# Attention row sums inverted on GpSimd by a power of minus one, and the convolution's first tap moved to ScalarE

## The chip, the cores and the metric

The kernel runs on one core of a Trainium2 chip. A core has a matrix engine (TensorE, PE in the profile, with its weight loads as PEld), VectorE (DVE), ScalarE (ACT), GpSimd (POOL) and SyncE (SP), which here issues nearly all DMAs. Each engine works through its own instruction list in order, and they wait for each other by semaphores. The metric is the device time of one execution in microseconds (us); lower is better.

## The reference

One layer of a hybrid encoder: sequence 1024, width 1024, float32. The input is normalised and modulated, projected once, and the columns go to two groups of heads: axial-rotary attention (8 heads of 64, two key/value heads) and a bidirectional mLSTM (4 heads of 128). Both are joined by an output projection; a SwiGLU feed-forward layer and a last norm follow. What the change touches is the softmax of the attention and the convolution ahead of the mLSTM:

```python
def one_block(q_blk):
    s = jnp.einsum('bkgqd,bksd->bkgqs', q_blk, kt).astype(jnp.float32) * scale
    p = jax.nn.softmax(s, axis=-1).astype(vt.dtype)
    return jnp.einsum('bkgqs,bksd->bkgqd', p, vt)

def centred_depthwise_conv(x, w, b):          # x: (B, S, 1024), width 5
    y = lax.conv_general_dilated(x, w[:, None, :], (1,), [(2, 2)],
            dimension_numbers=('NWC', 'WIO', 'NWC'), feature_group_count=ch)
    return y + b

qk = jax.nn.silu(centred_depthwise_conv(qk_pre, conv_w, conv_b))
```

## The kernel before, in words

**Precision.** PE multiplies rounded float32 operands. To keep accuracy every operand is split into a high part (rounded, on ACT) and a low part (the rest, a subtraction on POOL or DVE); a product is three matmuls (`mm3`, lines 298 to 300). Weights come by DMA into `wst`, and `whi` (ACT) and `wlo` (POOL) are made from them.

**Order.** All orders are fixed when the program is built. A planner (`Clock`) holds an estimated cost of every instruction and simulates the engines; `Clock.chain` runs a list of steps one behind the other, each when its predecessor is done by the estimate plus a delay, and an instruction is written into its engine's list at the moment the planner gets to it. All elementwise instructions go out through `Engine.emit`, so nearly all of them carry line 96 in the profile, and tile names tell them apart. In a chain, `bg` names for a step an engine that it waits to find free in the plan before it is issued. The planner prices a DVE `reciprocal` of one column at 0.07 us, a GpSimd `pow` at 0.1 us plus 0.21 per element and partition, a DVE `tensor_scalar` of 1024 with two column operands at 0.80, an ACT activation of that size with column scale and bias at 1.13 us.

**Streams.** PE's work is written as generators. In the attention stage the main ones are `values`, `turned` and `scores`; whenever none of them can go on in the plan, PE takes a step of the projection units (`units(IN)`), among them eight `conv_unit`s. Units that aren't done by the end of attention go on during the mLSTM stage.

**Attention.** There are 64 blocks (8 heads, 8 query tiles of 128). For one block:

- `scores` (line 978): PE makes S, 128 queries by 1024 keys, in PSUM (two buffers).
- `top`: DVE takes the row maximum into column 0 of the small tile `sst` and scales it into column 1.
- `exp`: ACT writes P (three buffers) in SBUF, with the row sum accumulated into column 2 (this ends with an ACTIVATION_READ_ACCUMULATOR).
- DVE's `reciprocal` writes column 3 of `sst`.
- `norm`: POOL multiplies P by that column, in place.
- `turned` (line 1010): PE transposes P in two halves into the PSUM tile T (two buffers); ACT copies the high part to PT, DVE subtracts the low part into PT.
- `values` (line 1029): for two blocks at a time PE multiplies PT by the values into `av`; ACT and DVE add its two halves (`avt`), and SP stores them.

**Queries.** Each head's queries are loaded (`qd`) and split into `qs` (ACT, then POOL).

**Convolution.** A `conv_unit` projects 128 channels of 1024 positions into `acc`, ACT copies them to `xp` (two zeros on each side), and then a chain runs: `tap(0)` makes `y` from `xp`, weight column and bias; `tap(1)` to `tap(4)` add the other shifted products on DVE; ACT's tanh and one DVE instruction make the SiLU; SP stores `y` to DRAM for the mLSTM. Between them DVE also takes the products for the modulation vector (`ada`).

Of the kernel before, what the change touches and what calls it, by code (L numbers as in the profile page):

```python
# [11 lines left out]
F32 = mybir.dt.float32  # L12
F32R = mybir.dt.float32r
BF16 = mybir.dt.bfloat16
AF = mybir.ActivationFunctionType
OP = mybir.AluOpType
# [4 lines left out]
P = 128  # L21
S = 1024
# [14 lines left out]
LAT = 0.14  # L37
# [203 lines left out]
def layer_kernel(ctx, tc, xT, c, w_ada, vecs, cons, rope, w_f, w_t0, w_t, w_o, w_gu, w_d, out):  # L241
    nc = tc.nc

    const = ctx.enter_context(tc.tile_pool(name="const", bufs=1))
# [5 lines left out]

    both = const.tile([P, 2], F32, name="both")
    mhalf, eps = both[:, 0:1], both[:, 1:2]
    nc.vector.memset(mhalf, -0.5)
    nc.vector.memset(eps, EPS)
    vec = const.tile([P, NVEC], F32, name="vec")
    nc.scalar.dma_start(vec, vecs)
# [3 lines left out]
    def V(n, i=0, w=1):  # L260
        o, _ = VEC[n]
        return vec[:, o + i:o + i + w]
# [39 lines left out]
    def dma(dst, src, q=None):  # L302
        (q or nc.sync).dma_start(dst, src)
        on_chip = dst.space == src.space == bass.MemoryType.SB if hasattr(src, "space") else False
        return ck.dma(math.prod(dst.shape) * 4, 0.65 if on_chip else 0.5)

    def halves(n):
        return slice(n * HALF, (n + 1) * HALF)

    ck = Clock()  # L310
    dve, act, gps = Engine(ck, nc.vector, "dve"), Engine(ck, nc.scalar, "act"), Engine(ck, nc.gpsimd, "gps")
# [28 lines left out]
    def psum_tile(shape, tag):  # L340
        t, bufs = PP["tags"][tag]
        f = Flag()
        PP["ring"].setdefault(t, []).append(f)
        return PP["ps"].tile(shape, F32, tag=t, name=tag, bufs=bufs), f
# [6 lines left out]
    with tc.manual_schedule():  # L351
# [351 lines left out]
        def tile_mms(w0, last):  # L703

            for n in range(NH):
                for k in range(KT):
                    yield [pieces[w0 + k // 4][2]] + ([slot("acc")] if k == 0 else [])
                    if k == 0:
                        acc, f = psum_tile([P, HALF], "acc")
                        open_sum[0] = True  # L710
                    mm3(acc, weights(w0, k, 4), (h_hi[k][:, halves(n)], h_lo[k][:, halves(n)]), k == 0, k == KT - 1)
                    ck.pe(0.65)
                    if n == 1 and k % 4 == 3:
                        load_piece()
                    if k == KT - 1:
                        open_sum[0] = False
                        last(n, acc, f)
# [13 lines left out]
        def conv_unit(i, w0):  # L731
            yield convs[-2:-1]
            prev = convs[-1:] if nbig[0] < 4 else []
            convs.append(mqk_ok[i])
            xp = bp.tile([P, S + 4], F32, tag="big", name="xp")
            gps.memset(xp[:, 0:2], 0.0)
            gps.memset(xp[:, S + 2:S + 4], 0.0)
            Y = []

            def tap(j):  # L740
                if j == 0:
                    Y.append(bp.tile([P, S], F32, tag="big", name="y"))
                    dve.tensor_scalar(Y[0], xp[:, 0:S], V("conv_w", i * 5), V("conv_b", i), op0=OP.mult, op1=OP.add)
                else:
                    dve.scalar_tensor_tensor(
                        Y[0], xp[:, j:j + S], V("conv_w", i * 5 + j), Y[0], op0=OP.mult, op1=OP.add)

            def tanh():
                act.activation(xp[:, 0:S], Y[0], AF.Tanh, scale=0.5)

            def silu():

                dve.scalar_tensor_tensor(Y[0], xp[:, 0:S], 1.0, Y[0], op0=OP.add, op1=OP.mult)

            def store():
                dma(mqk_d[i], Y[0])

            def last(n, acc, f):
                def evac():
                    act.activation(xp[:, 2 + n * HALF:2 + (n + 1) * HALF], acc, AF.Copy)  # L760

                e = ck.chain(LAT, evac, flag=f)
                if n == 1:
                    eng = ["dve"] * 5
                    ck.chain(LAT, e, *prev, *[lambda j=j: tap(j) for j in range(5)], tanh, silu, store,
                             flag=mqk_ok[i], bg=[None] * (1 + len(prev)) + eng + ["act", "dve", None])

            yield from tile_mms(w0, last)

        mqk_ok = [Flag() for _ in range(8)]  # L770
# [165 lines left out]
        def ada_late(last=48, ahead=2):  # L936

            n = len(adas)
            if n == 64 and all(f.done for f in adas[-2:]) and not summed:
                summed.append(1)  # L940
                mod_sum(40, 48)
            if n >= last or n >= ahead and not (adas[n - ahead].done and adas[n - ahead].t <= ck.t):
                return
            j, i = 16 + n // 2, n % 2
            t = PP["ada"].tile([P, HALF], F32, tag="ada", name="ada", bufs=ahead)
            adas.append(ck.chain(dma(t, w_ada[j][:, halves(i)]), lambda: dve.scalar_tensor_tensor(
                t, t, 1.0, PP["cond"][:, halves(i)], op0=OP.mult, op1=OP.mult, accum_out=modacc[:, i, j:j + 1])))
# [4 lines left out]
        Pok = [Flag() for _ in range(NQ)]  # L952
# [4 lines left out]
        def att_q(h):  # L957
            qd = ap.tile([P, S], F32, tag="qd", name="qd", bufs=1)
            src = q_d[h // 2][(h % 2) * DH:(h % 2 + 1) * DH]
            dma(qd[0:DH], src)  # L960
            arrive = dma(qd[DH:P], src)
            qs = ap.tile([P, S], F32R, tag="qs", name="qs")
            Q[h] = qs, ck.chain(arrive, lambda: act.activation(qs, qd, AF.Copy),
                                lambda: gps.tensor_sub(qs[DH:P], qd[DH:P], qs[DH:P].bitcast(F32)))

        def scores():

            for q in range(NQ):
                h, j = divmod(q, NJ)
                if j == 2 and h + 1 < AH:  # L970
                    att_q(h + 1)
                ada_late()
                g, (qs, ok) = h // 4, Q[h]
                yield [ok, k2_ok[g]] + [slot("S")] + Tem[max(q - 3, 0):max(q - 2, 0)]
                sp, f = psum_tile([P, S], "S")
                for n in range(NH):
                    for m in range(2):
                        nc.tensor.matmul(sp[:, halves(n)], qs[:, j * P:(j + 1) * P], k2[g][m][:, halves(n)],  # L978
                                         start=m == 0, stop=m == 1)
                ck.pe(0.87)  # L980
                st = ap.tile([P, 4], F32, tag="sst", name="sst", bufs=6)
                cq = colq[:, j, h:h + 1]

                def top(st=st, sp=sp, cq=cq):
                    dve.reduce_max(st[:, 0:1], sp, axis=AX.X)
                    dve.tensor_scalar(st[:, 1:2], st[:, 0:1], cq, -1.0, op0=OP.mult, op1=OP.mult)

                def exp(st=st, sp=sp, cq=cq, q=q, f=f):
                    Pt[q] = ap.tile([P, S], F32, tag="P", name="P", bufs=3)
                    act.activation(Pt[q], sp, AF.Exp, bias=st[:, 1:2], scale=cq, accum_out=st[:, 2:3])  # L990
                    f.set(ck, ck.fin + LAT)

                def norm(st=st, q=q):
                    gps.tensor_scalar(Pt[q], Pt[q], st[:, 3:4], 0.0, op0=OP.mult, op1=OP.add)

                ck.chain(LAT, top, exp, lambda st=st: dve.reciprocal(st[:, 3:4], st[:, 2:3]), norm, flag=Pok[q])

        def turned():

# [44 lines left out]
        Y = {}  # L1044
# [893 lines left out]
        psum_open("ps1", {"acc": ("acc", 1), "acct": ("acc", 1), "T": ("T", 2), "S": ("S", 2), "av": ("av", 1)})  # L1938
        att_q(0)
        ck.streams([Stream(values()), Stream(turned()), Stream(scores())], [un])  # L1940
        ck.streams([un], stop=lambda: convs[-1].done and len(convs) == 8 and not open_sum[0])
        while len(adas) < 48:
# [144 lines left out]
```

## Time and profile before

| what | value |
|---|---|
| median of 3 runs | 1405.1 us (1402.33 to 1405.69) |
| the profiled execution | 1407.29 us |
| its span, first to last instruction | 1405.5 us |
| mean granted TensorE clock | 0.972 |
| attention blocks, first maximum to last average | about 209 to 507 us |
| first taps of the eight convolutions | first at 191.1 us, last at 460.1 us |

The profile is of one execution. Busy time is given by engine; a group of instructions is one engine, operation and pair of tiles, with its count, busy time, mean in ns, the idle time of the engine just before it and what ended that. A wait is put down to whatever ended it last. "issue" is a wait for which the profile shows no cause. In time order a row gives start, duration, engine, line, operation and tiles, and in brackets the idle time before it.

### The profile page before, as it was taken

How to read it: one execution, taken by the hardware profiler on the slowest of the kernel's cores; microseconds unless marked ns; L12 is line 12 of the kernel's file. 1: busy time of each engine (PE TensorE's matmuls, PEld its weight loads, DVE VectorE, ACT ScalarE, POOL GpSimd, SP SyncE). 2: the span in 40 equal slices, each digit the busy share in tenths (PEclk: the TensorE clock that was granted, in tenths of full speed). 3: DMA queues.
4: the chain of work that ended last, by engine and by line, in shares of the span. 5: the costliest groups of instructions: out<-in, count | busy, mean ns of one | idle time of the engine just before them, and what ended most of it. 6: DMA issues, size and time to landing. Idle time of an engine off the chain costs nothing.

```text
span 1405.5 us, 19481 instructions
## 1 busy us (share of the span) xinstructions
PE 1300.5 (93%) x6594; PEld 1072.1 (76%) x6602; DVE 1065.1 (76%) x1600; ACT 662.9 (47%) x1194; POOL 679.0 (48%) x555
## 2 busy tenths in 40 slices
PE   5789798999999989899996999999999999979997
PEld 2578577889878979777774888888888887757887
DVE  7947979986788848768589886666666654798866
ACT  5454316677666655454476333332332334344463
POOL 5555554545344336577421355454544545545542
PEclk9899989999999999999998999999999999989999
DMA  7446462322122146553552333322332259723324
GB/s 287 165 128 203 135 172 80 108 77 65 38 65 70 35 140 211 188 203 115 196 187 75 113 120 105 107 104 100 110 113 90 71 175 327 275 81 102 93 65 154
DMA packets 103172, 184.40 MB, mean 131 GB/s; under 512 B 11296, under 2 KB 32672, under 8 KB 103072
## 3 DMA queue, kind: packets, MB, share of 16 engines
q1 hardware_dynamic: 89968, 161.06, 36.0%
q10 hardware_dynamic: 13104, 22.10, 4.2%
q8 instruction: 52, 0.85, 0.2%
q14 instruction: 48, 0.39, 0.1%
HBM read 136.19 MB, written 43.25 MB: 128 GB/s over the span
## 4 chain that ended last, share of the span: by engine, by line
PE 61%; DVE 20%; DMA 6%; issue 5%; ACT 3%; POOL 3%; SPq 1%; DVEq 0%; ACTq 0%; POOLq 0%
PE acc L299 15%; PE acc L298 15%; PE acc L300 15%; DVE x L96 3%; PE av L1029 3%; DVE ada L96 3%; DVE sst L96 2%; PE T L1010 2%; DVE PT L96 2%; PE S L978 2%; DVE y L96 1%; PE acct L298 1%; PE acct L300 1%; PE acct L299 1%; DVE wd L96 1%
## 5 line engine op out<-in xcount | busy, mean ns | idle before, releaser
L96 POOL TENSOR_TENSOR wlo<-wst,whi 128x512 fp32r<-128x512 f32 (+2 forms) x196 | 279.5, 1432 | 285.0 <-ACT whi L96 272.9
L96 ACT ACTIVATE whi<-wst 128x512 fp32r<-128x512 f32 (+2 forms) x219 | 131.0, 605 | 125.1 <-POOL wlo L96 25.3
L96 POOL TENSOR_SCALAR P<-P,sst 128x1024 f32<-128x1024 f32 x64 | 88.9, 1392 | 141.1 <-DVE sst L96 106.4
L299 PE MATMUL acc<-x,whi 128*128 128x512 f32 x352 | 140.7, 400 | 5.9 <-DVE x L96 5.9
L96 POOL TENSOR_TENSOR wlo<-wr,whi 128x512 fp32r<-128x512 f32 x56 | 76.9, 1374 | 77.4 <-ACT whi L96 73.9
L298 PE MATMUL acc<-hh,whi 128*128 128x512 f32 x224 | 97.5, 435 | 14.1 <-ACT hh L96 11.8
L298 PE MATMUL acc<-whi,wch 128*128 128x512 f32 x244 | 97.2, 398 | 6.3 <-ACT wch L96 6.3
L96 ACT ACTIVATE P<-S,sst,colq 128x1024 f32<-128x1024 f32 x64 | 77.3, 1207 | 52.4 <-DVE sst L96 47.9
L299 PE MATMUL acc<-hl,whi 128*128 128x512 f32 x224 | 92.4, 412 | 8.2 <-POOL hl L96 4.5
L300 PE MATMUL acc<-whi,wcl 128*128 128x512 f32 x244 | 97.2, 398 | 2.9 <-DVE wcl L96 2.8
L299 PE MATMUL acc<-wlo,wch 128*128 128x512 f32 x244 | 97.0, 398 | 0.6 <-POOL wlo L96 0.5
L96 DVE SCALAR_TENSOR_TENSOR ada<-ada,cond 128x512 f32<-128x512 f32 (+1 forms) x79 | 80.2, 1023 | 18.3 <-DMA ada<-in_w_ada_dram 12.7
L300 PE MATMUL acc<-hh,wlo 128*128 128x512 f32 x224 | 91.5, 409 | 0.0
L96 DVE TENSOR_TENSOR sg<-acc,sg 128x512 f32<-128x512 f32 x67 | 45.4, 687 | 58.8 <-PE acc L300 58.5
L96 ACT ACTIVATE PT<-T 128x512 fp32r<-128x512 f32 x128 | 71.4, 597 | 37.7 <-PE T L1010 36.9
L96 ACT ACTIVATE whi<-wr 128x512 fp32r<-128x512 f32 x60 | 37.9, 632 | 108.1 <-DVE wr L96 50.3
L96 DVE TENSOR_TENSOR PT<-T,PT 128x512 fp32r<-128x512 f32 x128 | 82.8, 681 | 7.2 <-ACT PT L96 7.1
L96 POOL TENSOR_TENSOR wlo<-s,whi 128x512 fp32r<-128x512 f32 x40 | 53.8, 1347 | 70.7 <-ACT whi L96 70.7
L299 PEld LDWEIGHTS acc<-x,whi 128*128 128x128 f32 x352 | 67.0, 190 | 22.3 <-DVE x L96 7.3
L298 PE MATMUL acct<-whi,hh 128*128 128x256 f32 (+1 forms) x256 | 79.4, 310 | 2.5 <-ACT xp L96 1.2
L96 DVE TENSOR_TENSOR wcl<-wd,wch 128x512 fp32r<-128x512 f32 x50 | 48.0, 972 | 42.1 <-ACT wch L96 26.9
L1010 PE MATMUL T<-con,P 128*128 128x128 f32 x512 | 70.3, 275 | 10.2 <-DVE PT L96 7.4
(459 smaller groups left out, 3802.5 us busy)
## 6 DMA issues: line engine op xcount, KB each, us to landing
wr<-in_w_gu_dram SPq DMA_DIRECT2D x66, 256.0 KB, 2.8
ada<-in_w_ada_dram SPq DMA_DIRECT2D x64, 256.0 KB, 3.3
wd<-in_w_d_dram SPq DMA_DIRECT2D x22, 512.0 KB, 7.0
wst<-in_w_gu_dram SPq DMA_DIRECT2D x34, 256.0 KB, 3.1
wst<-act_d SPq DMA_DIRECT2D x33, 256.0 KB, 4.1
ada<-in_w_ada_dram SPq DMA_DIRECT2D x16, 512.0 KB, 5.5
wst<-in_w_o_dram SPq DMA_DIRECT2D x32, 256.0 KB, 4.3
act_d<-sg ACTq DMA_DIRECT2D x31, 256.0 KB, 2.0
```

The lines of the kernel that those rows point to most:

```text
L96: return fn(*args, **kw)
L298: nc.tensor.matmul(acc, w[0], x[0], start=first, stop=False)
L299: nc.tensor.matmul(acc, w[0], x[1], start=False, stop=False)
L300: nc.tensor.matmul(acc, w[1], x[0], start=False, stop=last)
L978: nc.tensor.matmul(sp[:, halves(n)], qs[:, j * P:(j + 1) * P], k2[g][m][:, halves(n)], start=m == 0, stop=m == 1)
L1010: nc.tensor.transpose(tp[:, k], Pt[q][:, (4 * b + k) * P:(4 * b + k + 1) * P], ident)
L1029: nc.tensor.matmul(av, va[:, k, h // 4], PT[it][m][:, k], start=(k, m) == (0, 0), stop=(k, m) == (NJ - 1, 1))
```

## The change

A constant column of minus ones is made once. In the convolution, `tap(0)` is an ACT activation (identity, with the weight column as scale and the bias column as bias) in place of DVE's `tensor_scalar`, and in the chain it waits in the plan for ACT to be free instead of DVE. In the attention, the step between `exp` and `norm` is a GpSimd `tensor_tensor` that raises the row sum to the power of minus one, in place of DVE's `reciprocal`. As the planner prices the new instructions differently, the orders that it writes for all engines can differ from there on.

```diff
     both = const.tile([P, 2], F32, name="both")
     mhalf, eps = both[:, 0:1], both[:, 1:2]
+    mone = const.tile([P, 1], F32, name="mone")
     nc.vector.memset(mhalf, -0.5)
+    nc.vector.memset(mone, -1.0)
     nc.vector.memset(eps, EPS)
...
                 if j == 0:
                     Y.append(bp.tile([P, S], F32, tag="big", name="y"))
-                    dve.tensor_scalar(Y[0], xp[:, 0:S], V("conv_w", i * 5), V("conv_b", i), op0=OP.mult, op1=OP.add)
+                    act.activation(Y[0], xp[:, 0:S], AF.Identity, scale=V("conv_w", i * 5), bias=V("conv_b", i))
...
                 if n == 1:
-                    eng = ["dve"] * 5
+                    eng = ["act"] + ["dve"] * 4
...
-                ck.chain(LAT, top, exp, lambda st=st: dve.reciprocal(st[:, 3:4], st[:, 2:3]), norm, flag=Pok[q])
+                ck.chain(LAT, top, exp, lambda st=st: gps.tensor_tensor(st[:, 3:4], st[:, 2:3], mone, op=OP.pow),
+                         norm, flag=Pok[q])
```

## The prediction

> **What bounds the kernel now.** I read the page first, then the busy time by stretches, then what TensorE (PE) waits for in the attention stage, since both edits act only there. The page:
>
> ```profile
> span 1405.5 us, 19481 instructions
> PE 1300.5 (93%) x6594; PEld 1072.1 (76%) x6602; DVE 1065.1 (76%) x1600; ACT 662.9 (47%) x1194; POOL 679.0 (48%) x555
> ```
>
> PE is the busiest engine. The stretches 190 to 510 us hold all attention blocks and all eight convolutions (columns: PE, PEld, DVE, ACT, POOL busy, then granted clock, DMA share, GB/s):
>
> ```profile
> core 0: us, PE busy (x) PEld busy (x) DVE busy (x) ACT busy (x) POOL busy (x), PEclk, DMA share, GB/s
> 190.00:510.00 320.00, 302.63 (x1957) 263.85 (x1957) 269.29 (x448) 203.00 (x353) 140.51 (x104) 1.00 0.25 74
> 200.00:300.00 100.00, 90.89 (x569) 77.72 (x568) 95.77 (x162) 63.89 (x107) 51.13 (x33) 1.00 0.37 111
> 300.00:400.00 100.00, 98.17 (x650) 86.26 (x650) 72.97 (x132) 68.15 (x121) 42.46 (x39) 1.00 0.20 56
> 400.00:510.00 110.00, 104.31 (x703) 92.75 (x704) 90.89 (x145) 68.72 (x122) 43.27 (x31) 1.00 0.15 47
> ```
>
> PE is idle for 320.00 - 302.63 = 17.4 us. Nearly all of it lies where VectorE (DVE) is full: 9.1 us in 200:300 at 96% DVE, against 1.8 us in 300:400 at 73%. While attention is held up, PE does projection matmuls of the next units; a faster attention chain only moves those matmuls later, so PE's 302.6 us are work that stays. What a change here can win is at most the 17.4 us. Who owns them:
>
> ```profile
> engine line waited for: us in total, times, longest us
> PE T L1010 <- DVE PT L96: 7.4, 9, 2.0
> PE acc L298 <- ACT xp L96: 2.2, 4, 0.7
> PE T L1010 <- POOL P L96: 1.7, 4, 0.9
> PE S L978 <- ACT P L96: 1.4, 1, 1.4
> PE acct L298 <- ACT xp L96: 1.2, 1, 1.2
> PE av L1029 <- DVE PT L96: 1.0, 2, 0.5
> PE acct L298 <- DVE avt L96: 0.9, 1, 0.9
> ```
>
> 7.4 + 1.0 + 0.9 = 9.3 us wait for a DVE evacuation of PSUM (the low half of the transposed probabilities, PT, or the sum avt). 1.7 + 1.4 = 3.1 us wait for the softmax chain, where DVE's maximum and reciprocal stand. The reason shows in time order in the worst stall, DVE and POOL (GpSimd) first, then PE:
>
> ```profile
> 434.41 0.80 DVE L96 TENSOR_SCALAR y<-xp,vec 128x1024 f32<-128x1024 f32 x1
> 435.25 2.02 DVE L96 SCALAR_TENSOR_TENSOR y<-xp,vec,y 128x1024 f32<-128x1024 f32 x1
> 437.19 0.15 DVE L96 RECIPROCAL sst<-sst 128x1 f32<-128x1 f32 x1
> 437.59 3.02 DVE L96 SCALAR_TENSOR_TENSOR y<-xp,vec,y 128x1024 f32<-128x1024 f32 x1
> 440.53 0.68 DVE L96 TENSOR_TENSOR PT<-T,PT 128x512 fp32r<-128x512 f32 x1
> ...
> 436.36 3.16 POOL L96 TENSOR_TENSOR qs<-qd,qs 64x1024 fp32r<-64x1024 f32 x1
> ...
> 441.35 0.63 PE L1010 MATMUL T<-con,P 128*128 128x128 f32 x4 [2.03 <-DVE PT L96]
> ```
>
> Three convolution taps stand in DVE's queue ahead of PT, one of them 3.02 us long beside a POOL subtraction, and PE stops for 2.03 us. The order is fixed in the program; the stall is the real DVE lagging behind the planned one.
>
> **Part 1, what DVE loses.** The rows of what is removed and of what stays around it:
>
> ```profile
> L96 DVE TENSOR_SCALAR y<-xp,vec 128x1024 f32<-128x1024 f32 x8 | 8.7, 1090 | 2.2 <-ACT xp L96 2.2
> L96 DVE SCALAR_TENSOR_TENSOR y<-xp,vec,y 128x1024 f32<-128x1024 f32 x32 | 49.3, 1541 | 0.3
> L96 DVE SCALAR_TENSOR_TENSOR y<-xp,y 128x1024 f32<-128x1024 f32 x8 | 9.7, 1214 | 0.6 <-ACT xp L96 0.6
> L96 DVE RECIPROCAL sst<-sst 128x1 f32<-128x1 f32 x64 | 10.1, 158 | 24.8 <-ACT P L96 24.7
> ```
>
> 8 x 1.090 = 8.7 us of first taps and 64 x 0.158 = 10.1 us of reciprocals go: DVE falls from 269.3 to about 250 us. Besides, at 24 of the reciprocals DVE stood still until the exponential came, 24.7 us in all; that place in DVE's queue is gone. How much of the 9.3 us of PE's waits for DVE follows is not in the trace: 0 if the redrawn order spends the room on something else, 12.4 (9.3 + 3.1) if all goes. One wait is on average 7.4 / 9 = 0.82 us; a tap ahead of it is worth 0.8 to 1.1, a reciprocal 0.16. But a convolution is (8.7 + 49.3 + 9.7) / 8 = 8.5 us of DVE, and only 1.1 of that goes, so a backlog with taps two to five in it stays a backlog. I take a little under half of 9.3: **-4.0 us**.
>
> **Part 2, the reciprocal on POOL.** No trace row has a one-element power; the two nearest have 4 and 16 elements a partition (min/median/max ns):
>
> ```profile
> L96 POOL TENSOR_TENSOR ss<-ss,both x8: 1008/1012/1381, 546.6 to 667.1; 128x4 f32<-128x4 f32 x8
> L96 POOL TENSOR_TENSOR rqv<-rqv,both x4: 2920/3242/3349, 99.7 to 179.9; 128x16 f32<-128x16 f32 x4
> ```
>
> (2920 - 1008) / 12 = 159 ns an element, so 1008 - 3 x 159 = 0.53 us for one; bounds 0.1 (no fixed cost at all) and 1.0 (all fixed). I take 0.53, the line through both. 64 x 0.53 = 34 us take POOL from 140.5 to 174 of 320 us, 54%. On the chain a short-cut and a detour meet. Where DVE is free the old step cost 0.16 and a hop, and the new one is some 0.3 us longer; where DVE is behind, the old one waited for it. The start of attention shows the second:
>
> ```profile
> 203.45 1.98 DVE L96 TENSOR_SCALAR y<-xp,vec 128x1024 f32<-128x1024 f32 x1 [0.81 <-ACT xp L96]
> 205.47 3.52 DVE L96 SCALAR_TENSOR_TENSOR y<-xp,vec,y 128x1024 f32<-128x1024 f32 x2
> 208.91 1.21 DVE L96 TENSOR_REDUCE sst<-S 128x1 f32<-128x1024 f32 x1
> ...
> 211.58 0.19 ACT L96 ACTIVATION_READ_ACCUMULATOR P<-S,sst,colq 128x1 f32 x1
> ...
> 212.86 0.16 DVE L96 RECIPROCAL sst<-sst 128x1 f32<-128x1 f32 x1
> ...
> 213.12 2.58 POOL L96 TENSOR_SCALAR P<-P,sst 128x1024 f32<-128x1024 f32 x2 [2.98 <-DVE sst L96]
> ...
> 214.65 1.09 PE L1010 MATMUL T<-con,P 128*128 128x128 f32 x8 [0.94 <-POOL P L96]
> ```
>
> The sum is there at 211.77, the reciprocal waits 1.09 us for a tap. The power would end at about 211.80 + 0.53 and the product start at 212.36 instead of 213.12: 0.76 us off the 0.94 that PE waits. The second convolution's first tap there (1.98 us, stretched) becomes an ACT instruction; its end moves between 0.78 us earlier (start 203.45, 1.24 us long, next tap at 205.47 before) and 0.2 later (behind two weight copies). I take -0.3. Opening: **-1.0 us**. At the other blocks the detour costs nothing that I count: PE waited for a product only 4 times in 64, 1.7 us in all, because the transposes stand later in PE's order, behind other matmuls. If that cover were gone, 64 x 0.3 = 19 us would show. Behind the power on POOL stand the product, the weights' low halves (wlo) and qs; all waited behind the product before, and the power begins where the reciprocal did or earlier.
>
> **Part 3, the first tap on ScalarE (ACT).**
>
> ```profile
> L96 ACT ACTIVATE xp<-y 128x1024 f32<-128x1024 f32 x8 | 8.5, 1059 | 7.8 <-DVE y L96 5.2 <-DVE sst L96 2.6
> L96 ACT ACTIVATE hh<-x 128x512 fp32r<-128x512 f32 x16 | 9.8, 626 | 0.3
> L96 ACT ACTIVATE x<-x,mod,sc 128x512 f32<-128x512 f32 x32 | 25.4, 809 | 29.6 <-DVE x L96 29.6
> L96 ACT ACT_TABLE_LOAD x12 | 15.4, 1283 | 1.8 <-PEq L2075 1.6
> ```
>
> A 128x1024 activation without pointers takes 1.06 us; column scale and bias cost 0.809 - 0.626 = 0.18 more: 1.24 us, 9.9 us for eight, ACT from 203 to 213 of 320 us. The same function runs 32 times in this kernel on 12 table loads, so no load comes with it. Behind a tap on ACT stand the high half of PT, which DVE's low half and PE's T buffers wait for, and the exponentials. Bounds 0 (ACT is idle a third of the time, and the planner puts the tap where ACT is free) and +9.9 (each tap ahead of a PT that PE wants). I take **+0.8**, nearer the idle. A convolution finishes about as before; its store stays on SP's queue, and no DMA is moved.
>
> **Part 4, the two engines in each other's way.** Taps with two SBUF inputs stretch beside POOL work: 3.02 us beside the 3.16 us subtraction above, against a mean of 1.54. Powers are one more such neighbour, for 34 of 320 us: the 40 instructions on y, each with a chance of 34 / 320 = 0.11 and up to 0.53 us, make 40 x 0.11 x 0.53 = 2.3 us of DVE at most, and removing the first tap (up to 1.98 us at 203.45) takes eight such meetings away. **+0.5** on PE, between -1 and +2. The Trainium skill, SBUF — State Buffer, section "Who interferes with whom", says that a VectorE instruction with two SBUF inputs and a GpSimd one that reads SBUF exclude each other for a whole instruction, whoever came first, and that ScalarE never waits on anyone. That speaks against 64 more short GpSimd reads and for the moved tap; the trace agrees with the 3.02 us tap. Taking the rule alone, a power could wait out a whole tap, and the term would be nearer +2 than +0.5.
>
> The one-time constant on DVE at the start is under 0.2 us and is left out. **Sum:** -4.0 - 1.0 + 0.8 + 0.5 = -3.7 us. The profiled execution took 1407.3 us (span 1405.5 and 1.8 around it), so 1403.6; the median of the runs is 2.2 below it, 1405.1, so the same gain gives **1401.4 us**.
>
> **The rivals.** First, *nothing comes through*: the planner redraws all orders from the new costs, and the lag between plan and chip makes about as many new stalls; the same 17 us of idle stay. For it: PE is at 95% and the stalls are spread over 9 places; against: the DVE load really falls by 7%. 1405, give or take 3. Second, *all of DVE's share goes*: 9.3 + 3.1 = 12.4 us less; for it speaks 300:400, where DVE at 73% leaves 1.8 us idle; against, the taps two to five. 1393. Third, *slower*: the ACT tap is put, at each convolution, ahead of a PT high half; both T buffers are then held, PE's next transpose stops for what the tap lasts, 8 x 1.24 = 9.9 us, and DVE's gain shrinks to -3: 1412. It decides once PE's waits behind ACT and PT together pass about 13 us (8.4 now plus the gain). Against it: ACT at 63%. That the change does not do what it says (a table load at every tap and back, 8 x 2 x 1.28 = 20.5 us of ACT) would be the same case, worse; the 12 loads speak against it.
>
> **How the numbers follow.** Chances: forecast 0.45 (its own range 1397 to 1406), nothing 0.22, all of DVE's share 0.16, slower 0.17. A measurement of this kernel can tell about 0.3%, 4.2 us: faster means under 1400.9, slower over 1409.3. The forecast lies just above that line: 0.22 of it faster, 0.23 same. Faster 0.22 + 0.16 + 0.02 (from the first rival) = 0.40; same 0.23 + 0.17 = 0.40; slower 0.17 + 0.03 = 0.20. The range 1392 to 1412 reaches to both outer cases.
>
> **What would show it.** Step 1: DVE busy in the attention stage about 250 us, and PE's waits for DVE PT near 4 to 5 us instead of 7.4. Step 2: 64 powers on POOL of 0.4 to 0.6 us, and PE's waits for the product still under 3 us; the first transpose about 1 us earlier. Step 3: eight 128x1024 activations of about 1.24 us, 12 table loads as before, no new PE wait behind ACT PT. Step 4: the remaining taps' mean not above 1.6 us. Wrong would be: powers over 1 us with waits for the product, ACT taps followed by T stalls, or PE's idle in the stage unchanged although DVE's load fell.

## The result and the profile after

The changed kernel takes 1426.99 us (median of 4 runs, 1425.09 to 1428.56) against 1404.61 us before (4 runs): a ratio of 1.0157, 95% interval 1.0138 to 1.0175. It is slower by 22 us; 1401.4 was forecast, with a range up to 1412. The profiled execution took 1425.86 us, its span 18.6 us longer than that of before. The page after:

```profile
span 1424.1 us, 19529 instructions
PE 1305.4 (92%) x6602; PEld 1079.5 (76%) x6602; DVE 1050.4 (74%) x1529; ACT 670.2 (47%) x1202; POOL 705.8 (50%) x619
```

DVE has less to do, GpSimd and ScalarE a little more, as intended. The attention stage, in the same stretch as in the prediction, is not where the loss lies:

```profile
190.00:510.00 320.00, 306.99 (x1986) 269.37 (x1985) 253.59 (x370) 209.54 (x361) 171.66 (x168) 0.99 0.26 76
```

PE's idle time there fell from 17.4 to 320.00 - 306.99 = 13.0 us. So I cut both traces at the end of attention (the last `av` matmul) and at the end of the mLSTM (the last copy of its transposed output, `ymt`). Before (columns as in the prediction):

```profile
205.00:506.00 301.00, 285.92 (x1875) 250.39 (x1873) 255.18 (x429) 196.78 (x343) 134.39 (x101) 1.00 0.23 68
506.00:675.00 169.00, 153.71 (x904) 131.77 (x912) 119.67 (x272) 83.89 (x216) 111.62 (x148) 0.98 0.57 184
675.00:1405.00 730.00, 699.29 (x3098) 565.87 (x3098) 532.22 (x667) 294.00 (x500) 325.41 (x238) 0.98 0.40 131
```

After:

```profile
206.00:515.00 309.00, 297.62 (x1969) 263.08 (x1968) 243.85 (x360) 205.00 (x358) 169.67 (x169) 0.99 0.25 72
515.00:695.00 180.00, 146.47 (x816) 123.36 (x815) 119.23 (x271) 81.00 (x209) 104.87 (x145) 0.91 0.51 163
695.00:1424.00 729.00, 697.52 (x3105) 566.13 (x3104) 532.66 (x667) 294.56 (x500) 324.07 (x238) 0.98 0.40 132
```

Attention is 8 us longer with 94 matmuls more in it (x1875, x1969). The mLSTM stage is 11 us longer although PE has 88 matmuls fewer to do in it: its idle time rose from 169.00 - 153.71 = 15.3 to 180.00 - 146.47 = 33.5 us. The rest is unchanged. What moved is projection work into attention: the matmuls of the last projection units (tile `acct`), with which PE fills its gaps, called filling matmuls below. Attention holds 312 of them before and 405 after (401 up to the last `av` matmul itself). Before:

```profile
205.00:506.00 301.00, 52.68 (x312) 43.60 (x312) 0.00 (x0) 4.96 (x13) 1.00 0.23 68
```

After:

```profile
206.00:515.00 309.00, 60.83 (x405) 53.59 (x406) 0.00 (x0) 6.07 (x16) 0.99 0.25 72
```

Where PE stands still in the mLSTM stage after the change, by its waits:

```profile
PE ni L1817 <- DVE num L96: 17.4, 9, 9.7
PE acc L300 <- ACT yah L96: 6.1, 1, 6.1
```

Before, the first of these was 6.9 us in four waits. The second, near the stage's end, is for an operand of the output projection; it was not followed. The longest wait, 9.7 us, in time order: DVE's list after the change around 555 us, and PE's next instruction.

```profile
550.80 0.60 DVE L96 SCALAR_TENSOR_TENSOR num<-ni,cols,num 128x130 f32<-128x130 f32 x2
555.30 1.72 DVE L96 SCALAR_TENSOR_TENSOR ada<-ada,cond 128x512 f32<-128x512 f32 x1 [3.90 <-DMA ada<-in_w_ada_dram]
...
559.66 0.78 DVE L96 SCALAR_TENSOR_TENSOR ada<-ada,cond 128x512 f32<-128x512 f32 x1 [0.97 <-DMA ada<-in_w_ada_dram]
...
564.98 0.69 DVE L96 SCALAR_TENSOR_TENSOR ada<-ada,cond 128x512 f32<-128x512 f32 x1 [1.07 <-DMA ada<-in_w_ada_dram]
...
565.88 0.61 DVE L96 SCALAR_TENSOR_TENSOR num<-ni,cols,num 128x130 f32<-128x130 f32 x2
...
566.64 1.21 PE L1817 MATMUL ni<-Cs,mq 128*128 128x260 f32 x2 [9.69 <-DVE num L96]
```

From 551.4 to 565.9 DVE does nothing for the mLSTM. Six products of modulation columns (`ada`) stand in its list in one block, most of them waiting for a weight column to come by DMA, and the sum `num`, for which PE waits, stands behind them. The code that writes such a block belongs to neither edit; it stands behind the stage in which the last projection units fill PE's gaps:

```python
ck.streams(mem, [un], stop=lambda: un.wait is None and all(f.done for v in vo_ok for f in v))
while not summed:
    ck.need(*adas[-2:])
    ada_late(64)
```

Once the projection units are done, the planner stops every stream until the last modulation columns have come, because the buffers of both are given up next. This stop is called the halt below. Before, the units were done last and the loop had nothing to wait for. The row of the units' last copies (vstg, first and last start) and of the column products, before:

```profile
L96 ACT ACTIVATE vstg<-acct x32: 364/385/390, 96.8 to 582.2; 128x256 f32<-128x256 f32 x32
L96 DVE SCALAR_TENSOR_TENSOR ada<-ada,cond x79: 654/685/2877, 22.6 to 556.3; 128x512 f32<-128x512 f32 x64, 128x1024 f32<-128x1024 f32 x15
```

After:

```profile
L96 ACT ACTIVATE vstg<-acct x32: 361/383/386, 97.7 to 551.5; 128x256 f32<-128x256 f32 x32
L96 DVE SCALAR_TENSOR_TENSOR ada<-ada,cond x79: 654/693/2874, 22.2 to 565.0; 128x512 f32<-128x512 f32 x64, 128x1024 f32<-128x1024 f32 x15
```

The order has turned round: units 582 and columns 556 before, units 551 and columns 565 after.

### The profile page after: what moved, and what is told of

It reads as the page before. It is cut to its first block, busy times and chain, and to the rows that moved or that the text cites. A ratio compares the mean times of both kernels' runs of the same rounds, so it can differ in the third digit from the quotient of the medians.

```text
span 1424.1 us, 19529 instructions
## 1 busy us (share of the span) xinstructions
PE 1305.4 (92%) x6602; PEld 1079.5 (76%) x6602; DVE 1050.4 (74%) x1529; ACT 670.2 (47%) x1202; POOL 705.8 (50%) x619
## 4 chain that ended last, share of the span: by engine, by line
PE 59%; DVE 14%; issue 5%; DMA 3%; POOL 3%; ACT 2%; SPq 0%; DVEq 0%; ACTq 0%; POOLq 0%
PE acc L301 15%; PE acc L302 15%; PE acc L300 15%; PE av L1032 3%; DVE sst L96 3%; PE T L1013 2%; PE S L980 2%; DVE x L96 2%; DVE PT L96 2%; DVE y L96 1%; DMA ada<-in_w_ada_dram 1%; DVE Cs L96 1%; PE ni L1817 1%; DVE ada L96 1%; DVE s L96 1%
## 5 line engine op out<-in xcount | busy, mean ns | idle before, releaser
L96 POOL TENSOR_TENSOR wlo<-wst,whi 128x512 fp32r<-128x512 f32 (+2 forms) x196 | 277.4, 1422 | 291.0 <-ACT whi L96 285.3
L96 POOL TENSOR_TENSOR sst<-sst,mone 128x1 f32<-128x1 f32 x64 | 44.3, 692 | 117.6 <-ACT P L96 112.7
L96 DVE TENSOR_REDUCE sst<-S 128x1 f32<-128x1024 f32 x64 | 77.7, 1215 | 6.3 <-PE S L980 5.5
L96 POOL TENSOR_SCALAR P<-P,sst 128x1024 f32<-128x1024 f32 x64 | 77.7, 1214 | 6.3
```

The lines of the kernel that those rows point to most:

```text
L96: return fn(*args, **kw)
```

## The experiments

The planner keeps a clock of its own while it writes the program. Read out at some points, it gives for each kernel (us of the planner's clock; the chip's median beside it):

```
                                 attention ends  halt   mLSTM ends  end      chip
before                           426.2           0      568.9       1241.0   1405
both parts (the change)          438.6           20.7   597.7       1271.1   1427.0
power only                       432.0           0      574.3       1247.7   1414.2
tap only                         427.7           0      570.4       1242.6   1401.8
change, no halt                  438.6           0      573.0       1245.1   1407.1
change, last unit held           438.3           1.1    571.6       1245.0   1402.3
change, last two units held      435.4           0      594.2       1267.6   1426.3
change, more columns early       441.7           0      578.7       1252.1   1418.4
change, no halt, one unit early  435.1           0      569.8       1241.9   1403.1
```

**The power alone.**

```diff
-                    act.activation(Y[0], xp[:, 0:S], AF.Identity, scale=V("conv_w", i * 5), bias=V("conv_b", i))
+                    dve.tensor_scalar(Y[0], xp[:, 0:S], V("conv_w", i * 5), V("conv_b", i), op0=OP.mult, op1=OP.add)
...
-                    eng = ["act"] + ["dve"] * 4
+                    eng = ["dve"] * 5
```

> The reciprocal is GpSimd's power, the first tap stays on DVE. Theory A (the time is lost through the orders that the planner redraws: with both parts it lets one more projection unit run inside the attention stage, and the mLSTM stage lacks it): the planner's own end here is 6.7 us later than before and no extra unit is pulled in (with both parts its end is 30.1 us later), so about 1410 us (1406 to 1415), far from 1427. Rival B (the power itself, in GpSimd's queue and in the softmax chain, costs the time): 1420 us or more, most of the 22 us.

1414.21 us, ratio 1.0061 (1.0041 to 1.0081). Slower by about 8 us, a good third of the loss, as theory A had it. Attention ends at 511.6 us here and at 505.9 before, 5.7 later; the planner has 5.8 (432.0 against 426.2).

**The tap alone.**

```diff
-                ck.chain(LAT, top, exp, lambda st=st: gps.tensor_tensor(st[:, 3:4], st[:, 2:3], mone, op=OP.pow),
+                ck.chain(LAT, top, exp, lambda st=st: dve.reciprocal(st[:, 3:4], st[:, 2:3]),
```

> The first tap is on ScalarE, the reciprocal stays on DVE. Theory A: the planner's end is 1.6 us later than before, so 1404 us give or take 4. Rival B (each tap on ScalarE holds back the high halves): about 1412 us, 8 x 1.24 us more, less DVE's gain.

1401.77 us, ratio 0.9968 (0.9950 to 0.9986): faster by 4 us. The two parts alone come to +8 - 4 = +4; together they cost 22. The difference of 18 belongs to neither part alone.

**Both parts, written in the order of before.** An instruction goes out on its new engine, while the planner books the old one.

```diff
+    def planned(eng, cost, emit):
+        ck.run(eng, cost)
+        emit()
...
-                    act.activation(Y[0], xp[:, 0:S], AF.Identity, scale=V("conv_w", i * 5), bias=V("conv_b", i))
+                    planned("dve", 0.07 + 0.63 + 0.05 * 2, lambda: nc.scalar.activation(
+                        Y[0], xp[:, 0:S], AF.Identity, scale=V("conv_w", i * 5), bias=V("conv_b", i)))
...
-                    eng = ["act"] + ["dve"] * 4
+                    eng = ["dve"] * 5
...
-                ck.chain(LAT, top, exp, lambda st=st: gps.tensor_tensor(st[:, 3:4], st[:, 2:3], mone, op=OP.pow),
+                ck.chain(LAT, top, exp, lambda st=st: planned(
+                    "dve", 0.06 + 6.5 / 1024, lambda: nc.gpsimd.tensor_tensor(st[:, 3:4], st[:, 2:3], mone, op=OP.pow)),
```

> Both parts on their new engines, but the planner is told that they are DVE's reciprocal and DVE's tap as before, so that it writes the orders of before (the same plan to the last hundredth). Theory A: the loss is gone, and what DVE was relieved of shows: 1402 us (1398 to 1406). Rival B (the instructions themselves cost the time on GpSimd and ScalarE): about 1425 us.

1403.16 us, ratio 0.9974 (0.9959 to 0.9988). The loss is gone. Attention and the mLSTM hold as many matmuls as before (x1875, x904) and take as long within 1 us (301 and 169 us before):

```profile
205.00:507.00 302.00, 287.83 (x1875) 253.49 (x1873) 244.46 (x360) 202.94 (x351) 170.19 (x166) 0.99 0.23 68
507.00:677.00 170.00, 155.41 (x904) 133.28 (x912) 119.34 (x272) 83.52 (x215) 111.34 (x149) 0.97 0.57 183
```

**The old engines, written in the order of the change.**

```diff
-                    act.activation(Y[0], xp[:, 0:S], AF.Identity, scale=V("conv_w", i * 5), bias=V("conv_b", i))
+                    planned("act", 0.1 + 0.85 + 0.09 * 2, lambda: nc.vector.tensor_scalar(
+                        Y[0], xp[:, 0:S], V("conv_w", i * 5), V("conv_b", i), op0=OP.mult, op1=OP.add))
...
-                ck.chain(LAT, top, exp, lambda st=st: gps.tensor_tensor(st[:, 3:4], st[:, 2:3], mone, op=OP.pow),
+                ck.chain(LAT, top, exp, lambda st=st: planned(
+                    "gps", 0.1 + 0.21, lambda: nc.vector.reciprocal(st[:, 3:4], st[:, 2:3])),
```

> The reverse: reciprocal and tap stay on DVE, but the planner is told that they are GpSimd's power and ScalarE's tap, so that it writes the orders of the changed kernel. Theory A: 1428 us (1423 to 1434), with 60 or so more projection matmuls inside the attention stage and PE idle some 33 us between the end of attention and the end of the mLSTM. Rival B: about 1405 us.

1429.55 us, ratio 1.0159 (1.0135 to 1.0184). The whole loss is there with no power and no ScalarE tap in the program. Attention holds 402 filling matmuls, 90 more than before (some 60 more were expected), and the stage after it is like that of the change (519 to 699 us):

```profile
519.00:699.00 180.00, 146.23 (x813) 122.72 (x820) 119.19 (x271) 81.26 (x210) 105.67 (x146) 0.91 0.51 163
```

With the run before it this settles the first question: in the order of before the new instructions gain 0.26%, and it is the redrawn order that loses. What in the order is to blame was still open: the halt (theory A1), or merely that the mLSTM has less filling work (rival A2). The other five runs are on the changed kernel.

**No halt.**

```diff
+        ck.streams(mem, stop=lambda: bool(summed))
         while not summed:
```

> The changed kernel, but where the planner stops every stream until the last modulation columns have come (the loop on `summed` before the output projection is opened), the mLSTM's streams may go on. The attention stage is planned as in the changed kernel, with the same 401 or so projection matmuls in it. Theory A1 (the projection units end early, the planner halts for 20.7 us of its own clock at that loop, DVE's list gets the last columns' products in one block ahead of the mLSTM's sums, and PE waits behind them): the halt is gone, the planner's end falls from 1271.1 to 1245.1, so 1407 us (1402 to 1413). Rival A2 (the mLSTM simply has too few projection matmuls left to fill its gaps): 1422 us or more.

1407.14 us, ratio 0.9996 (0.9984 to 1.0009). One line takes the loss away. Attention is as in the changed kernel, with the same x1969 matmuls, and the mLSTM stage is 19 us shorter. PE's idle time in it falls from 33.5 to 161.00 - 142.81 = 18.2 us, and its busy time by 3.7 us for nearly as many matmuls (x816, x810), at a granted clock of 0.98 in place of 0.91:

```profile
206.00:515.00 309.00, 297.43 (x1969) 263.19 (x1967) 243.77 (x362) 204.70 (x357) 168.88 (x168) 0.99 0.24 71
515.00:676.00 161.00, 142.81 (x810) 121.02 (x816) 118.90 (x271) 79.81 (x209) 108.22 (x146) 0.98 0.57 184
```

The units still end before the columns (551 and 568 us here), but DVE's list now has the columns one or two at a time, the mLSTM's sums between them:

```profile
553.80 0.61 DVE L96 SCALAR_TENSOR_TENSOR num<-ni,cols,num 128x130 f32<-128x130 f32 x2 [0.36 <-ACT num L96]
554.33 0.80 DVE L96 SCALAR_TENSOR_TENSOR ada<-ada,cond 128x512 f32<-128x512 f32 x1
...
556.19 0.60 DVE L96 SCALAR_TENSOR_TENSOR num<-ni,cols,num 128x130 f32<-128x130 f32 x2
...
560.90 1.09 DVE L96 SCALAR_TENSOR_TENSOR ada<-ada,cond 128x512 f32<-128x512 f32 x1
...
561.92 0.60 DVE L96 SCALAR_TENSOR_TENSOR num<-ni,cols,num 128x130 f32<-128x130 f32 x2
```

**The last projection unit held** until attention has ended (a unit from piece 40 on waits for a flag that is set there).

```diff
+        HOLD = []
...
             for kind, i in order:
+                if HOLD and start[kind, i] >= HOLD[0]:
+                    yield [HOLD[1]]
...
         att_q(0)
+        HOLD[:] = [40, Flag()]
         ck.streams([Stream(values()), Stream(turned()), Stream(scores())], [un])
+        HOLD[1].set(ck, ck.t)
```

> The changed kernel, with the last projection unit kept back until attention has ended; the unit before it still runs inside attention, so some 384 of the 401 matmuls of the changed kernel stay there. Theory A1: the last unit then ends late enough that the columns are there (the planner halts for 1.1 us instead of 20.7, its end is 1245.0), so 1407 us (1402 to 1413). Rival A2: hardly any filling work is given back to the mLSTM (some 18 matmuls, 2 us), so 1422 us or more.

1402.28 us, ratio 0.9976 (0.9965 to 0.9988). Only about 18 filling matmuls changed place, and 25 us went: the units now end when the columns do (last starts at 559.6 and 560.7 us), as theory A1 has it; rival A2's 1422 us or more is out. The forecast was 5 us too high; why this run is faster than the one without a halt was not followed.

**The last two units held**: the same with 36 in place of 40.

> The changed kernel, with the last two projection units kept back until attention has ended: more filling work for the mLSTM than in the kernel before (all 384 matmuls of the two instead of some 264). Rival A2: the mLSTM is full again, 1405 us or less. Theory A1 adds that the planner's clock, which has no halt here, is a forecast for the chip: its attention stage is only 3 us shorter than the changed kernel's, since PE then idles between the blocks, and its end is 1267.6, so about 1422 us (1415 to 1430).

1426.26 us, ratio 1.0139 (1.0121 to 1.0156). The mLSTM has more filling work than before, and the kernel is as slow as the change, without any halt: rival A2's 1405 us is out. Attention, with 192 filling matmuls, takes as long as with 405, PE idling for 309.00 - 282.12 = 26.9 us in it (its waits for DVE PT are 16.3 us there), and the work kept back makes the mLSTM stage 181 us long:

```profile
206.00:515.00 309.00, 282.12 (x1755) 243.85 (x1753) 244.02 (x360) 202.18 (x346) 165.56 (x166) 0.97 0.23 65
515.00:696.00 181.00, 165.23 (x1018) 144.59 (x1027) 116.21 (x271) 86.30 (x221) 108.78 (x148) 0.98 0.54 174
```

```profile
PE T L1013 <- DVE PT L96: 16.3, 15, 2.3
```

**More columns during attention.**

```diff
-                ada_late()
+                ada_late(56)
```

> The changed kernel, with eight more modulation columns (56 instead of 48 half columns) loaded and multiplied during attention, so that fewer are left for the mLSTM stage. Theory A1: no halt at the loop (the columns are there when the projection units end), the planner's end is 1252.1, so 1413 us (1407 to 1419). Rival A2: no filling work is given back, 1422 us or more.

1418.4 us, ratio 1.0082 (1.0067 to 1.0098): the halt is gone from the plan, 8.6 us come back, and the rest doesn't; attention ends at 524.6 us here, 10 us later than in the change, and PE's waits for DVE PT between 190 and 510 us are 9.9 us (5.7 in the change). A cure with a price, 5 us above its forecast. What makes those waits longer was not followed.

**No halt, and one unit earlier** among the projection units (t2 behind the first convolution).

```diff
-IN = ([("t", 0), ("q", 1), ("q", 2), ("q", 3), ("f", 0), ("f", 4), ("f", 1), ("f", 5), ("t", 2), ("f", 2), ("f", 6),
-       ("f", 3), ("f", 7), ("t", 1), ("t", 3)])
+IN = [("t", 0), ("q", 1), ("q", 2), ("q", 3), ("f", 0), ("t", 2), ("f", 4), ("f", 1), ("f", 5), ("f", 2), ("f", 6), ("f", 3), ("f", 7), ("t", 1), ("t", 3)]
...
+        ck.streams(mem, stop=lambda: bool(summed))
         while not summed:
```

> The changed kernel without the planner's halt (as in the run that lets the mLSTM's streams go on) and with one token-major projection unit moved ahead among the projection units (t2 behind the first convolution). The planner's end is 1241.9, 3.2 below that run's 1245.1 and 0.9 above the kernel before's 1241.0. Theory A1 (the planner's end, halts included, tells the chip's time to some 4 us): 1402 us (1397 to 1407), at best a little under the kernel before. Rival A2: still some 400 filling matmuls inside attention, so 1422 us or more.

1403.07 us, ratio 0.9973 (0.9962 to 0.9985). It beats both kernels by little: 0.3% below before. It, the tap alone, the order of before and the last unit held lie within each other's intervals; which of them is best is not settled.

## Why the prediction was wrong

**What bounds the kernel.** The step that failed is the bound drawn from it: "PE's 302.6 us are work that stays", so what a change here can do is at most the 17.4 us of idle, and the redrawn order stands in the sum at nothing. The first half held in one run: without the halt, 94 matmuls more in attention make that stage 8 us longer and the mLSTM stage 8 us shorter (161 us against 169), for the same total. But I took it that the work may move freely. It may not: where the filling work ends decides whether a loop behind attention finds the modulation columns there, and with two units held back attention was no shorter for their absence. The halt turned a harmless move into 19 us (180 us of mLSTM stage with it, 161 without), beside 20.7 us in the planner's clock. The trace of before held the margin, which I did not read: the last projection copies at 582.2 us, the last column product at 556.3. Before, 264 filling matmuls were left at the end of attention and the last of these copies came 76 us later; in the change 174 were left and it came 37 us later (551.5), while attention itself ended 9 us later. So the units ended 31 us earlier, which is more than the 26 us of margin.

**The first rival** was the nearest, "the planner redraws all orders from the new costs", but I gave it "give or take 3" without a source for the 3. The redraw was worth +24 us either way: with the old engines 1429.55 in the new order against 1405.93 in the old, with the new engines 1426.99 against 1403.16. The halt is some 20 of these 24 us (1426.99 against 1407.14); what makes the remaining 4 stays open. The slower rival had the right sign for the wrong cause: ScalarE's taps hold nothing back; alone the moved tap makes the kernel 0.3% faster.

**Part 1** was right in kind. DVE fell to 253.6 us (some 250 forecast). PE's waits for DVE PT fell from 7.4 to 5.7 us, where 4 to 5 was forecast. The stage after the change, by PE's waits:

```profile
PE T L1013 <- DVE PT L96: 5.7, 11, 1.1
PE T L1013 <- POOL P L96: 3.1, 2, 2.7
PE av L1032 <- DVE PT L96: 0.6, 1, 0.6
```

**Part 2** sized the power rightly and lost the opening. Undisturbed it takes 0.54 us (0.53 forecast; the lower bound of 0.1 was wrong, as the forecast's own slope gives 0.16), but its mean is 0.69, and the longest is 1.52:

```profile
L96 POOL TENSOR_TENSOR sst<-sst,mone x64: 537/546/1519, 212.9 to 504.4; 128x1 f32<-128x1 f32 x64
```

The first power is such a long one. I had it run at once and the product start 0.76 us sooner; after the change it stands beside a DVE tap:

```profile
212.71 1.28 DVE L96 SCALAR_TENSOR_TENSOR y<-xp,vec,y 128x1024 f32<-128x1024 f32 x1
...
212.87 1.51 POOL L96 TENSOR_TENSOR sst<-sst,mone 128x1 f32<-128x1 f32 x1 [1.69 <-ACT P L96]
...
214.49 2.20 POOL L96 TENSOR_SCALAR P<-P,sst 128x1024 f32<-128x1024 f32 x1
...
216.75 1.58 PE L1013 MATMUL T<-con,P 128*128 128x128 f32 x8 [2.70 <-POOL P L96]
```

The tap that held the reciprocal in DVE's queue now holds the power through the memory that both read, and the next tap seems to do the same to the product (2.20 us against a median of 1.13): PE waits 2.70 us there instead of 0.94. The term of -1.0 us should have been about +1.8. In the order of before the first power takes 1.51 us too, and PE waits 0.93 us there: nothing was won. The other 63 products were hidden as forecast: 3.1 us of waits in all, 2.7 of them this one.

**Part 3** was right: eight activations of 1.248 us, 12 table loads as before, and no wait of PE on a high half of PT among the waits of the stage.

**Part 4** had the right effect in the wrong place. The 32 taps that stayed grew shorter, not longer (1442 ns in the mean, 1541 before), but the eight last steps of the SiLU (`y` from `xp` and `y`), which the forecast counted among its 40 instructions, grew from 1214 to 1555 ns. Together the 40 took 58.5 us, 59.0 before; what was held besides were the powers and the first product.

**The sum** of -3.7 us can be compared with the run that keeps the order of before: a ratio of 0.9974 is -3.7 us (-5.8 to -1.7). That the two agree is in part luck, and the trace does not show the gain where it was forecast. In that order attention ends at 506.1 us and the mLSTM at 676.3, against 505.9 and 674.7 before; the 2.4 us between the two profiled spans lie behind both, where neither edit acts (726.8 us against 730.8). PE's waits did move, but against each other:

```profile
PE T L1019 <- POOL P L96: 4.0, 3, 2.4
PE T L1019 <- DVE PT L96: 3.6, 5, 1.7
```

The waits for DVE PT fell from 7.4 us, as part 1 had it, and those for the product rose from 1.7, which part 2 put at nothing. The tap alone, with no power, gained as much (0.9968). For the program that was built the order was a term of its own, six times as large as the sum, and it was not in it.

## What to carry to other kernels

Where a planner writes the order, an edit is two changes: the instructions, and the order that their prices lead to. They can be told apart on the chip by writing each in the order of the other. And before a price is touched, look for places where the plan stops everything for a condition, and read from the trace how much slack each has: here the last projection copy came 26 us behind the last column.

## What the runs showed of the hardware

Two things were larger than expected. A one-element GpSimd power beside a DVE instruction with two inputs in SBUF takes up to 1.52 us instead of 0.54; of the 64 in the changed kernel 21 took over 0.65 us. Of these 21, 20 end 0.39 to 0.42 us behind the end of such a DVE instruction that had started before them; the other stands beside two taps that the trace shows as one row. The Trainium skill, SBUF — State Buffer, section "Who interferes with whom", has it that the later of the two waits for the earlier one's end; the rows agree, the first power's end being 0.4 us behind the tap's. So a step that leaves DVE's queue for GpSimd can meet the same DVE instruction again there.

And PE's long stall came with a lower granted clock: in the slice below, which holds most of the 9.7 us, it was half. In the next 10 us, with PE busy throughout, it was 0.89. Over the mLSTM stage it was 0.91 with the halt and 0.98 without, where PE took 3.7 us less for nearly the same work.

```profile
560.00:570.00 10.00, 3.36 (x10) 2.92 (x11) 6.46 (x21) 1.04 (x3) 1.80 (x2) 0.50 0.78 238
```
